# Dilated attention and gated linear attention block on one core: the rest transpose put into the bank of the fourth turned tile, the low-rank weights loaded during gk, and four smaller edits

## The chip, the cores and the metric

The kernel runs on one core of a Trainium2 chip. Time is device microseconds (us) of one execution, the median of 3 runs; lower is better. In tables of the profile, PE is the matrix engine, PEld its weight loads, DVE the vector engine, ACT the scalar engine, POOL the GpSimd engine and SP the engine that only issues DMAs here.

## What is computed

One layer over 512 tokens of width 2048, in float32. An adaLN-modulated RMSNorm gives `h`. One projection of `h` is cut into attention q, k, v and gate, and into q, k, v, gate and low-rank decay inputs of a gated linear attention (GLA):

```python
h = rms_norm(x) * (1.0 + scale[:, None]) + shift[:, None]
proj = h @ w_in[layer]
aq, ak, av, ag, gq, gk, gv, gg, lr_f, lr_b = jnp.split(proj, PROJ_SPLITS, axis=-1)
for window, dilation in DILATED_PATTERNS:        # (128,1), (512,4), (2048,16); 16 heads x 64
    o_p, lse_p = dilated_window_attention(aq, ak, av, rel_bias, window, dilation)
...
att = jnp.einsum('pbsh,pbshe->bshe', mix_w.astype(av.dtype), jnp.stack(outs, axis=0))
a_out = att.reshape(B, S, ATT_WIDTH) * jax.nn.silu(ag)
log_g_f = (jax.nn.log_sigmoid((lr_f @ gla_gate_up_fwd[layer] + ...)) / GLA_GATE_NORM).reshape(ks_)
o_fwd = gla_chunked(gq, gk, gv, log_g_f)         # and o_bwd on flipped inputs; 4 heads, dk 128, dv 256
g_out = rms_norm(o_fwd + o_bwd) * gla_norm_gain * silu(gg)
y = jnp.concatenate([a_out, g_out], axis=-1) @ w_out[layer]
x = x + gate[:, None] * y                        # then rms_norm(x) * final_gain
```

## The kernel before

**Products.** Every large product of float32 numbers is made of three products of rounded ones: each operand is split into a high part (rounded to fp32r, by ACT) and a low part (the difference, by DVE), and PE multiplies high by high, low by high and high by low (`three`, L229 to L232). The work is a sequence of *units*: `sta` and `stb` (L591 on: the first projections), `qk2`, `qk4`, `qk6` and `gk` (64 product steps of three matmuls of 512 columns each), `V` (the GLA values, by seven block products), `ag0`, `ag1`, `gg0`, `gg1` (gates), and the output projection `O` (seven block products, twice). Weights come by DMA from SP into raw tiles and are split as above (`split_hi` L493, `split_lo` L477).

**Order.** PE's order is the program's order, since its queue is scheduled by hand. A unit takes a list of side jobs, pairs of a fraction and a function; a job is emitted when the unit's product steps reach that fraction. DVE, ACT, POOL and SP are ordered by the scheduler, which makes each wait for the last instruction that used the same tile. All engines run their own queue strictly in that order.

**The front.** Before `sta` the condition is spread by eight products (`pc`), and PE then runs bridging products whose results nobody uses: `warm(n)` (L293 to L296) multiplies a tile of ones, `warm(5)` at the start and `warm(6)` behind the spread.

**Attention.** Side jobs of `qk2`, `qk4`, `qk6` and `gk`: four heads in each unit, four query tiles a head. `score(h, i)` (L829) makes two products into a bank `s{h}{i}`, adds the bias and finds the maximum (DVE, L847), takes exponentials (ACT, L851), a reciprocal (DVE, L854) and scales the row (POOL, L864). The probabilities then have to be transposed: `turn(h, i)` (L868) makes three PE transposes of 128x128 into a bank `t{h}{i}` (L882), whose result is split into `pth` (ACT, L888) and `ptl` (DVE, L889). Each query tile has 416 keys, three blocks of 128 and a rest of 32; the four rests of a head lie together in 128 columns of the head's first tile and are turned at once by `rest(h)` (L896): one PE transpose (L899), whose four strips of 32 partitions go to four places of `pth` and `ptl` by four ACT copies (L906) and four DVE subtractions (L908), in two pairs. `rest(h)` is called by `turn(h, 3)`, ahead of its three transposes. `values(h)` (L910) multiplies by v, nine matmuls into a bank `o{h}` (L915).

**PSUM.** There are eight banks of 512 float32 columns: a ring of five, `PJ` (L214), and a ring of three, `PA` (L217). A unit holds four of the `PJ` banks for its products. The fifth is shared by `r{h}`, the turned rests, and `o{h}`; the `PA` banks are taken in turn by `s{h}{i}` and `t{h}{i}`.

**Behind attention.** The low-rank weights are loaded into `lrb` (L1303) and split into `lrs` (ACT L1306, DVE L1307) behind the unit `gk`; their sixteen pairs of products run in the unit `V`. One GLA head each runs beside `V`, `ag0`, `ag1` and `gg0` (`gla_head`, L1012): `gates`, `turn` (three transposes, `kt`, L1062), `states` (three products `kv`, L1074), `att`, `outs` (`go`, L1123) and `norm`, at the fractions `GLA_AT`, or `GLA_FIRST` for head 0. Behind `gg1`, DVE combines blocks of the gated results for the output stage, `to_s1` and `to_s2` (L1471, L1474). The output stage loads half its raw weight tiles into a pool of its own (`out_tile`, L394).

Of the kernel before, what the change touches and what calls it, by code (L numbers as in the profile page):

```python
# [10 lines left out]
F32 = mybir.dt.float32  # L11
# [7 lines left out]
P = 128  # L19
S = 512  # L20
D = 2048
KT = D // P
# [95 lines left out]
REST_OF = (14, 11, 2, 15)  # L118
TOKENS = [slice(256 * c + a, 256 * c + 256, 2) for a in range(2) for c in range(2)]

GLA_AT = (0.01, 0.02, 0.33, 0.46, 0.46, 0.56, 0.64, 0.76, 0.76, 0.88)
GLA_FIRST = (0.3, 0.38, 0.55, 0.62, 0.775, 0.81, 0.86, 0.9, 0.92, 0.97)

SUMS_IN = {"ag0": 8, "ag1": 8, "gg0": 8}

# [66 lines left out]
def block_kernel(ctx: ExitStack, tc: tile.TileContext, a: dict):  # L192
    nc = tc.nc
# [14 lines left out]
    def T2(name, dt=F32, parts=P):  # L208
        return t2.tile([parts, 512], dt, tag="t2", name=name)
# [4 lines left out]
    def PJ(name):  # L214
        return pp.tile([P, 512], F32, tag="pj", bufs=5, name=name)

    def PA(name):  # L217
        return pp.tile([P, 512], F32, tag="pa", bufs=3, name=name)
# [74 lines left out]
    def warm(n):  # L293

        for _ in range(n):
            mm(psw, hot[:, :P], hot, start=True, stop=True)  # L296
# [4 lines left out]
    with tc.manual_schedule(engines=PLANNED):  # L301
        small_inputs()
        cond_load(0, 0)
        half_load(0)
        x_load(0)
        half_load(1)
        nc.scalar.preload_act_table_set("silu_and_others")
        nc.vector.memset(hot.bitcast(F32), 1.0)
        nc.vector.memset(epst, EPS)
        nc.vector.memset(ch.bitcast(F32), 0.0)  # L310
        nc.vector.memset(sel.bitcast(F32), 0.0)
        nc.gpsimd.memset(cl.bitcast(F32), 0.0)
        warm(5)

        nc.vector.tensor_copy(ch[:4], cin[:, :512])
        act(sel[:4], cin[:, 512:], AF.Copy)
        tt(cl[:4], cin[:, :512], ch[:4].bitcast(F32), op=ALU.subtract)

        nc.vector.tensor_scalar(bcond[:, 16:32], bcond[:, 16:32], 1.0, None, op0=ALU.add)
        for j in range(4):  # L320
            spread(j, ch, True)
            spread(j, cl, False)
            act(sb[:, 512 * j:512 * j + 512], pcs[j], AF.Silu)
        warm(6)

    def cond_sum(dst, w, with_, init):

# [65 lines left out]

    def out_tile(s, name):  # L394
        if s % 2 and s >= OUT_DEEP:
            return op.tile([P, 2, 512], F32, tag="raw", bufs=3, name=name)
        return RAW(name, [2, 512])

    second = {}
# [418 lines left out]
    def attention(pairs):  # L818
# [49 lines left out]
        def turn(h, i):  # L868
            def go():
                if not pts:  # L870
                    for z in "hl":
                        pts.append(B8(f"pt{z}", [16, P], F32R))
                        for at, to in ((2, 3), (11, 12)) + ((14, 16),) * (z == "h"):
                            nc.gpsimd.memset(pts[-1][:, at:to, :].bitcast(F32), 0.0)
                if i == 3:
                    rest(h)
                t = pr_.pop((h, i)) if i else pr_[h, i]
                pk = PA(f"t{h}{i}")
                first_ = 0 if i % 2 else 128
                for n_, (c, _) in enumerate(FULL[i]):  # L880
                    kt = (c - i - 1) % 4
                    nc.tensor.transpose(pk[:, n_ * P:n_ * P + P], t[:, first_ + kt * P:first_ + kt * P + P], ident)  # L882
                at, step = FULL[i][0][1], FULL[i][1][1] - FULL[i][0][1]
                hi, lo = (pt[:, at:at + 2 * step + 1:step, :] for pt in pts)
                src = pk[:, :3 * P].rearrange("p (k q) -> p k q", k=3)

                def parts():
                    act(hi, src, AF.Copy)  # L888
                    tt(lo, src, hi.bitcast(F32), op=ALU.subtract)  # L889
                if i or h == heads[0]:  # L890
                    parts()
                else:
                    held_parts.append(parts)
            return go

        def rest(h):  # L896

            pk = PJ(f"r{h}")
            nc.tensor.transpose(pk[:, :P], pr_.pop((h, 0))[:, 0:128], ident)  # L899
            hi, lo = pts  # L900
            to = [(hi, 0, hi, 32), (hi, 0, lo, 0), (hi, 96, lo, 96), (hi, 64, hi, 96)]
            parts = [(t[a:a + 32, REST_OF[i], :], u[b:b + 32, REST_OF[i], :], pk[96 - 32 * i:128 - 32 * i, :P])
                     for i, (t, a, u, b) in enumerate(to)]
            for pair in (parts[:2], parts[2:]):
                for up, _, of in pair:
                    act(up, of, AF.Copy)  # L906
                for up, low_, of in pair:
                    tt(low_, of, up.bitcast(F32), op=ALU.subtract)  # L908
# [103 lines left out]
    def gla_head(h):  # L1012
# [4 lines left out]
        def gates(d):  # L1017
            def go():
                n = f"{h}{d}"
                bias = gbias[:, 4 * d + h:4 * d + h + 1]  # L1020
                pz = PA("z" + n)
                mm(pz, gla["up"][:, d, h * P:h * P + P], gla["lr"], start=True, stop=True)
                e = T2("e" + n)
                act(e, pz, AF.Abs, bias=bias)
                act(e, e, AF.Exp, scale=-1.0)
                act(e, e, AF.Ln, bias=1.0)
                g = T2("g" + n)
                nc.vector.tensor_scalar(g, pz, bias, 0.0, op0=ALU.add, op1=ALU.min)  # L1028
                tt(g, g, e, op=ALU.subtract)
                b = T2("b" + n)  # L1030
                rst = gla["rst"]
                if d == 0:
                    nc.vector.tensor_tensor_scan(b, rst, g, 0.0, op0=ALU.mult, op1=ALU.add)
                    im, il = 63, 127
                else:
                    nc.vector.tensor_tensor_scan(b[:, ::-1], rst, g[:, ::-1], 0.0,
                                                 op0=ALU.mult, op1=ALU.add)
                    im, il = 64, 0
                b3 = b.rearrange("p (n t) -> p n t", n=4)
                sc = gs.tile([P, 3, 4], F32, tag="sc", name="sc" + n, bufs=4)  # L1040
                act(sc[:, 0, :], b3[:, :, im], AF.Exp, scale=1.0 / 16)
                act(sc[:, 1, :], b3[:, :, il], AF.Exp, scale=1.0 / 16)
                bm = T2("bm" + n)
                bm3 = bm.rearrange("p (n t) -> p n t", n=4)
                tt(bm3, b3, b3[:, :, im:im + 1].to_broadcast([P, 4, P]), op=ALU.subtract)
                act(sc[:, 2, :], bm3[:, :, il], AF.Exp, scale=1.0 / 16)
                qi = T2("qi" + n)
                ki = T2("ki" + n)
                act(ki, bm, AF.Exp, scale=-1.0 / 16)
                act(qi, bm, AF.Exp, scale=1.0 / 16)  # L1050
                gq, gk = gla["q"][:, h, :], gla["k"][:, h, :]
                tt(ki, ki, gk, op=ALU.mult)
                tt(qi, qi, gq, op=ALU.mult)
                dirs[d].update(qi=qi, ki=ki, sc=sc, order=[0, 1, 2] if d == 0 else [3, 2, 1])
            return go

        def turn(d):
            def go():
                n, x = f"{h}{d}", dirs[d]
                pk = PA("kt" + n)  # L1060
                for j, c in enumerate(x["order"]):
                    nc.tensor.transpose(pk[:, j * P:j * P + P], x["ki"][:, c * P:c * P + P], ident)  # L1062
                x["kit"] = T2("kit" + n)
                act(x["kit"][:, :384], pk[:, :384], AF.Copy)
            return go
# [65 lines left out]
        def norm():  # L1131
# [10 lines left out]
            for v in range(2):  # L1142
                m = 2 * h + v
                if m % 4 == 0:
# [2 lines left out]
                    op0=ALU.mult, op1=ALU.mult)  # L1147

        at = GLA_AT if h else GLA_FIRST
        return list(zip(at, [gates(0), gates(1), turn(0), turn(1), states(0), states(1), att,  # L1150
                             outs(0), outs(1), norm]))

    def urgent(go):
# [137 lines left out]
        for q in range(2):  # L1291
            qk_evict(p + 2 + q, ps[2 * q], ps[2 * q + 1])

    ps = unit("gk", False, attention((6, 7)))
    kp_.close()
    gs = mid.enter_context(tc.tile_pool(name="gs", bufs=1, reuse_waits="tile"))
    gla["k"] = B8("gkt", [4, 512])
# [1 line left out]
        act(gla["k"][:, i, :], ps[i], AF.Copy)  # L1299


    lrb = T2("lrb")
    nc.sync.dma_start(lrb.rearrange("p (k c) -> p k c", k=KT), a["w_lr"][0])  # L1303
    lrs = gp.tile([P, KT, 2, 32], F32R, tag="g", name="lrs")
    lrb3 = lrb.rearrange("p (k c) -> p k c", k=KT)
    act(lrs[:, :, 0, :], lrb3, AF.Copy)  # L1306
    tt(lrs[:, :, 1, :], lrb3, lrs[:, :, 0, :].bitcast(F32), op=ALU.subtract)  # L1307
    plr = PA("plr")
# [161 lines left out]
    def to_s1(z):  # L1470
        tt(part(z, 1), part(2 + z, 1), part(z, 1), op=ALU.subtract)  # L1471

    def to_s2(z):
        stt(part(z, 0), part(z, 1), -1.0, part(z, 0), op0=ALU.mult, op1=ALU.subtract)  # L1474
# [6 lines left out]
            (0.65, lambda: to_s1(0)), (0.8, lambda: to_s2(0))]  # L1481
    ps = unit("gg1", False, side + some_sums("gg1"))
    gate_evict(ps, cat[3], "g1")
    to_s1(1)
    to_s2(1)
    mid.close()
    op = ctx.enter_context(tc.tile_pool(name="op", bufs=1, reuse_waits="tile"))
    for e in "hl":
# [145 lines left out]
    def later(pair, prod, g, go):  # L1634
        todo.setdefault((pair, prod, g), []).append(go)
# [37 lines left out]
    for z in range(2):  # L1673
        later(0, "P4", 1 + 2 * z, lambda z=z: halves("A12", z, part(2 + z, 0))())
    later(0, "P1", 1, gate_row)
    later(0, "P4", 2, gain_rows(0))
    later(0, "P4", 3, x_again(0))
    later(1, "P7", 0, x_again(1))
# [129 lines left out]
```

## Time and profile before

| | |
|---|---|
| median of 3 runs | 905.07 us (904.97 to 905.77) |
| the profiled execution | 907.22 us, span 905.4 us, mean granted PE clock 0.996 |
| busy share of the span | PE 98%, PEld 82%, DVE 81%, ACT 54%, POOL 14% |
| DMA | 242.33 MB, mean 268 GB/s |

The profile is of one execution. A page of it gives busy times by engine, the chain of work that ended last and the costliest groups of instructions; the trace behind it can be asked for one engine's waits, for the instructions in a stretch of time, and for the busy times of all engines in given stretches, with the clock that PE was granted there (1.00 is full speed).

### The profile page before, as it was taken

Reading aid. Unit: us, or ns where it says so; the run is one execution under the profiler, and the core shown is the slowest. Engines: PE = TensorE matmul, PEld = TensorE weight load, DVE = VectorE, ACT = ScalarE, POOL = GpSimd, SP = SyncE. Lnnn points to the kernel's source line nnn. Section 1 sums busy time; section 2 is a strip of 40 time slices with the busy share of each in tenths; the row PEclk is TensorE's granted clock in tenths of the full one; section 3 lists DMA queues with packets and bytes.
Section 4 is the critical chain, followed back from the end, with each engine's and each line's share of the span. In section 5 each row is a group of like instructions: output and inputs, shape, how many; then the busy total and the mean of one; then the engine's idle time right before and its main releaser. Section 6 shows DMA issues by size and latency. Waiting matters only on the chain.

```text
span 905.4 us, 12339 instructions
## 1 busy us (share of the span) xinstructions
PE 890.0 (98%) x4159; PEld 739.2 (82%) x4159; DVE 731.2 (81%) x1220; ACT 491.6 (54%) x841; POOL 125.9 (14%) x219
## 2 busy tenths in 40 slices
PE   8999999999999999999999999999999999999996
PEld 6888788888888888887778888888888888888885
DVE  7998799878989989888568668595787559797687
ACT  5554533466655745655657554373664248455454
POOL 0000000023323333243000101112020100000001
PEclk9999999999999999999999999999999999999999
DMA  9999489398798898998778879778796988777863
GB/s 342 401 411 363 186 344 367 134 306 226 202 266 273 247 265 247 249 298 223 232 260 255 311 206 308 206 249 262 231 279 208 275 286 289 282 288 249 289 238 154
DMA packets 65547, 242.33 MB, mean 268 GB/s; under 512 B 9190, under 2 KB 11526, under 8 KB 55883
## 3 DMA queue, kind: packets, MB, share of 16 engines
q1 hardware_dynamic: 58724, 199.23, 61.5%
q0 software_dynamic: 6464, 42.01, 19.4%
q8 instruction: 33, 0.54, 0.2%
q10 hardware_dynamic: 296, 0.30, 0.1%
q14 instruction: 30, 0.25, 0.1%
HBM read 224.64 MB, written 51.47 MB: 305 GB/s over the span
## 4 chain that ended last, share of the span: by engine, by line
PE 91%; DVE 3%; ACT 2%; DMA 2%; issue 1%; SPq 0%; DVEq 0%; ACTq 0%
PE ps_qk L230 5%; PE ps_qk L232 5%; PE ps_qk L231 5%; PE g L232 4%; PE g L230 4%; PE g L231 4%; PE stb L232 3%; PE stb L231 3%; PE stb L230 3%; PE ps_ag L232 3%; PE ps_ag L230 3%; PE ps_ag L231 3%; PE o L915 3%; PE sta L230 3%; PE sta L231 3%; PE sta L232 3%
## 5 line engine op out<-in xcount | busy, mean ns | idle before, releaser
L864 POOL TENSOR_SCALAR p<-p,st 128x32 f32<-128x32 f32 (+2 forms) x108 | 59.8, 565 | 159.9 <-DVE st L854 91.2
L328 DVE CUSTOM_DVE_ANT_0 cb<-cb,sb,c_bcond 128x2048 f32<-128x2048 f32 (+1 forms) x32 | 73.4, 2295 | 1.9 <-DMA cb<-in_wm 1.6
L851 ACT ACTIVATE p<-p,st 128x416 f32<-128x416 f32 x64 | 41.0, 641 | 49.2 <-DVE st L847 42.3
L429 POOL DMA_DIRECT2D T<-in_w_o x32 | 23.2, 725 | 159.4 <-ACT V2h L493 14.8
L888 ACT ACTIVATE pth<-t 128x384 fp32r<-128x384 f32 x64 | 31.0, 485 | 19.8 <-PE t L882 11.1
L889 DVE TENSOR_TENSOR ptl<-t,pth 128x384 fp32r<-128x384 f32 x64 | 35.2, 551 | 5.2 <-ACT pth L888 3.7
L882 PE MATMUL t<-c_ident,p 128*128 128x128 f32 x192 | 31.3, 272 | 0.0
L882 PEld LDWEIGHTS t<-c_ident,p 128*128 128x128 f32 x192 | 24.3, 139 | 7.9
L847 DVE CUSTOM_DVE_ANT_0 p<-s,g,st 128x256 f32<-128x256 f32 x64 | 27.7, 432 | 1.8
L847 DVE CUSTOM_DVE_ANT_0 p<-s,g 128x160 f32<-128x160 f32 x64 | 23.5, 367 | 4.2 <-PE s L840 3.5
L328 DVE CUSTOM_DVE_ANT_0 rawg<-rawg,crow,gate 128x1024 f32<-128x1024 f32 x16 | 20.4, 1279 | 4.0 <-DMA rawg<-in_wg 4.0
L1581 POOL TENSOR_SCALAR x<-x,rn 128x512 f32<-128x512 f32 x2 | 2.3, 1167 | 148.5 <-ACT rn L1570 148.5
L429 POOL DMA_DIRECT2D T3V<-in_w_gv x8 | 5.5, 687 | 125.1 <-ACT qk21h L493 118.7
L839 PE MATMUL s<-ks,qh 128*128 128x416 f32 x64 | 22.6, 353 | 0.0
L906 ACT ACTIVATE pth<-r 32x128 fp32r<-32x128 f32 x64 | 17.2, 269 | 9.9 <-PE r L899 4.5
L840 PE MATMUL s<-ks,ql 128*128 128x416 f32 x64 | 22.4, 350 | 0.0
L1091 ACT ACTIVATE sq<-st,sc 128x256 f32<-128x256 f32 x24 | 12.2, 506 | 18.6 <-DVE st L1081 10.0
L328 DVE CUSTOM_DVE_ANT_0 rawg<-rawg,crow,c_bcond 128x1024 f32<-128x1024 f32 x16 | 20.3, 1279 | 0.5 <-DVE g L1028 0.5
L429 POOL DMA_DIRECT2D T<-T x16 | 9.1, 571 | 79.9 <-ACT V8h L493 12.9
L915 PE MATMUL o<-pth,vv 128*128 128x512 f32 (+1 forms) x64 | 15.9, 369 | 2.2 <-DVE pth L908 1.1
L466 DVE TENSOR_TENSOR raw_O<-raw_O,raw_P 128x1024 f32<-128x1024 f32 x8 | 9.8, 1225 | 10.1 <-DMA raw_O<-in_w_o 7.8
L568 ACT ACTIVATE h_hi<-xt,shift 128x512 fp32r<-128x512 f32 x16 | 11.5, 721 | 10.3 <-DVE shift L328 9.5
(1661 smaller groups left out, 3151.6 us busy)
## 6 DMA issues: line engine op xcount, KB each, us to landing
cb<-in_wm SPq DMA_DIRECT2D x31, 1024.0 KB, 9.3
T<-in_w_o POOLq DMA_DIRECT2D x32, 512.0 KB, 6.5
rawg<-in_wg SPq DMA_DIRECT2D x32, 512.0 KB, 5.4
raw_O<-in_w_o SPq DMA_DIRECT2D x32, 512.0 KB, 4.6
raw_qk<-in_w_qk SPq DMA_DIRECT2D x24, 512.0 KB, 4.9
raw_O<-T SPq DMA_DIRECT2D x24, 512.0 KB, 5.0
rawb<-in_w_sb SPq DMA_DIRECT2D x16, 512.0 KB, 8.9
rawv<-in_wv SPq DMA_DIRECT2D x16, 512.0 KB, 5.6
```

Of the source, the lines that this page charges most:

```text
L230: mm(ps, lh, rh, start=first, stop=False, skip_group_check=more)
L231: mm(ps, ll, rh, start=False, stop=False, skip_group_check=more)
L232: mm(ps, lh, rl, start=False, stop=last, skip_group_check=more)
L328: return nc.vector.tensor_tensor_reduce(out=w, in0=w, in1=with_, op0=ALU.mult, op1=ALU.add, scale=1.0, scalar=init, accum_out=dst)
L429: move = nc.gpsimd.dma_start(dst, src, max_dma_last_dim=8192, **how).ins
L847: top = nc.vector.tensor_tensor_reduce(out=t[:, lo:hi], in0=ps[:, lo:hi], in1=gt[h][:, at:at + 2 * (hi - lo) - 1:2], op0=ALU.add, op1=ALU.min,
L851: act(t, t, AF.Exp, bias=st[:, 0:1], scale=-1.0, accum_out=st[:, 1:2])
L864: last["pool"] = nc.gpsimd.tensor_scalar(to, of, st[:, 2:3], 1.0, op0=ALU.mult, op1=ALU.mult).ins
L882: nc.tensor.transpose(pk[:, n_ * P:n_ * P + P], t[:, first_ + kt * P:first_ + kt * P + P], ident)
L888: act(hi, src, AF.Copy)
L889: tt(lo, src, hi.bitcast(F32), op=ALU.subtract)
L915: mm(po[:, P * a0:P * a1], vv[h // 4][:, c, h % 4, :], pt[:, at:at + (a1 - a0 - 1) * step + 1:step, :], start=n_ == z == 0, stop=False, sk ...
```

## The change

Six edits:

1. `rest` writes its transpose into the last quarter of the bank `t{h}3`, which `turn(h, 3)` now takes first; the bank `r{h}` is no longer used. The code's order stays: the rest's transpose, its eight evictions, then the three transposes of the tile.
2. `lrb` is loaded by a side job of `gk` at 0.7 in place of behind `gk`.
3. The bridging products behind the spread are thirteen in place of six.
4. In a GLA head, `states(0)` comes ahead of `turn(1)`, whose fraction is 0.47 in place of 0.46; for head 0 the two `outs` come at 0.91 and 0.93 in place of 0.90 and 0.92.
5. `to_s1(1)` and `to_s2(1)` are emitted within the first block product of the output stage, in place of ahead of it.
6. The output stage's own raw tiles are four in place of three.

```diff
-GLA_AT = (0.01, 0.02, 0.33, 0.46, 0.46, 0.56, 0.64, 0.76, 0.76, 0.88)
-GLA_FIRST = (0.3, 0.38, 0.55, 0.62, 0.775, 0.81, 0.86, 0.9, 0.92, 0.97)
+GLA_AT = (0.01, 0.02, 0.33, 0.46, 0.47, 0.56, 0.64, 0.76, 0.76, 0.88)
+GLA_FIRST = (0.3, 0.38, 0.55, 0.775, 0.62, 0.81, 0.86, 0.91, 0.93, 0.97)
...
-        warm(6)
+        warm(13)
...
-            return op.tile([P, 2, 512], F32, tag="raw", bufs=3, name=name)
+            return op.tile([P, 2, 512], F32, tag="raw", bufs=4, name=name)
...
+                pk = PA(f"t{h}{i}")
                 if i == 3:
-                    rest(h)
+                    rest(h, pk[:, 3 * P:])
                 t = pr_.pop((h, i)) if i else pr_[h, i]
-                pk = PA(f"t{h}{i}")
...
-        def rest(h):
-
-            pk = PJ(f"r{h}")
-            nc.tensor.transpose(pk[:, :P], pr_.pop((h, 0))[:, 0:128], ident)
+        def rest(h, pk):
+
+            nc.tensor.transpose(pk, pr_.pop((h, 0))[:, 0:128], ident)
...
-            parts = [(t[a:a + 32, REST_OF[i], :], u[b:b + 32, REST_OF[i], :], pk[96 - 32 * i:128 - 32 * i, :P])
+            parts = [(t[a:a + 32, REST_OF[i], :], u[b:b + 32, REST_OF[i], :], pk[96 - 32 * i:128 - 32 * i, :])
...
-        return list(zip(at, [gates(0), gates(1), turn(0), turn(1), states(0), states(1), att,
+        return list(zip(at, [gates(0), gates(1), turn(0), states(0), turn(1), states(1), att,
                              outs(0), outs(1), norm]))
...
-    ps = unit("gk", False, attention((6, 7)))
+    def lr_load():
+        lrb.append(T2("lrb"))
+        nc.sync.dma_start(lrb[0].rearrange("p (k c) -> p k c", k=KT), a["w_lr"][0])
+
+    ps = unit("gk", False, attention((6, 7)) + [(0.7, lr_load)])
...
-    to_s1(1)
-    to_s2(1)
...
+    later(0, "P1", 1, lambda: (to_s1(1), to_s2(1)))
```

What the edits do to the order on the engines shows best at two places. The first is PE in the unit `gk`, at head 12's rest and fourth turned tile; `ps_gk` are the unit's products, `p` the probabilities, and a number behind a name tells one buffer from another. The brackets name the engines' counters that the instruction waits for. Before:

```order
L232 MATMUL ps_gk_3671<-h_lo,gk3h 128x512
L899 MATMUL r_3894<-c_ident,p_3734 128x128 [waits Pool_49]
L882 MATMUL t_3904<-c_ident,p_3817 128x128 [waits DVE_49,PE_49,Activation_49]
L882 MATMUL t_3904<-c_ident,p_3817 128x128 x2
L230 MATMUL ps_gk_3672<-h_hi,gk3h 128x512
```

And after:

```order
L232 MATMUL ps_gk_3666<-h_lo,gk3h 128x512
L898 MATMUL t_3889<-c_ident,p_3729 128x128 [waits DVE_49,PE_49,Pool_49]
L882 MATMUL t_3889<-c_ident,p_3812 128x128 [waits DVE_49,Activation_49]
L882 MATMUL t_3889<-c_ident,p_3812 128x128 x2
L230 MATMUL ps_gk_3667<-h_hi,gk3h 128x512
```

The sequence of PE's work is the same, but the rest's transpose now writes the tile of the three that follow, and it is the rest's transpose that waits for the bank's former users. The count of DVE's counter for which the first of the three waits is, after, that of the last of the four rest subtractions of the same head (L907 there); this is so in all 16 heads. Before, it was that of an earlier user of the bank `t`.

The second place is DVE's queue in the same head. Before:

```order
L854 RECIPROCAL st_3873<-st_3873 128x1 [waits Activation_49]
L908 TENSOR_TENSOR pth<-r_3894,pth 32x128 [waits PE_49,Activation_49]
L908 TENSOR_TENSOR ptl<-r_3894,pth 32x128
L889 TENSOR_TENSOR ptl<-t_3904,pth 128x3x128 [waits Activation_49]
L847 ISA p_3916,st_3917<-s_3913,g_3751 128x160 [waits PE_49,Pool_49]
L847 ISA st_3917 128x1
L908 TENSOR_TENSOR ptl<-r_3894,pth 32x128 [waits Activation_49]
L847 ISA p_3916,st_3917<-s_3913,g_3751,st_3917 128x256 [waits DVE_49]
L847 ISA st_3917 128x1
L908 TENSOR_TENSOR pth<-r_3894,pth 32x128
```

And after:

```order
L854 RECIPROCAL st_3868<-st_3868 128x1 [waits Activation_49]
L907 TENSOR_TENSOR pth<-t_3889,pth 32x128 [waits PE_49,Activation_49]
L907 TENSOR_TENSOR ptl<-t_3889,pth 32x128
L907 TENSOR_TENSOR ptl<-t_3889,pth 32x128 [waits Activation_49]
L907 TENSOR_TENSOR pth<-t_3889,pth 32x128
L889 TENSOR_TENSOR ptl<-t_3889,pth 128x3x128 [waits Activation_49]
```

The four subtractions of the rest now stand together, ahead of that of the three blocks (L889) and of the next tile's bias; on ACT the four copies stand together in the same way. The third place is ACT's queue where the low-rank weights are split. Before, in head 15:

```order
L906 ACTIVATE pth<-r_4296 32x128 [waits PE_49]
L906 ACTIVATE pth<-r_4296 32x128
L1306 ACTIVATE lrs<-lrb 128x16x32 [waits DMAHW3_49,DMAHW2_49]
L888 ACTIVATE pth<-t_4306 128x3x128 [waits PE_49]
L906 ACTIVATE pth<-r_4296 32x128 [waits DVE_49]
```

And after, where it stands between heads 14 and 15:

```order
L888 ACTIVATE pth<-t_4124 128x3x128 [waits PE_49,Activation_49]
L1309 ACTIVATE lrs<-lrb 128x16x32 [waits DMAHW6_49,DMAHW3_49]
L493 ACTIVATE V0h<-raw_V_4069 128x1024 [waits PE_49]
L851 ACTIVATE p_4138,st_4139<-p_4138,st_4139 128x416 [waits DMAHW1_49,DVE_49,Pool_49]
```

The split of the low-rank weights has moved ahead by most of a head. Its load on SP moved with it, from behind the load of `raw_V6` to just behind that of `raw_V4`. POOL's order is the same; `to_s1(1)` and `to_s2(1)` stand on DVE where the scheduler had put them before.

More of the change, by code (lines that the diff above doesn't have):

```diff
@@ L1292, in block_kernel @@
             qk_evict(p + 2 + q, ps[2 * q], ps[2 * q + 1])
-    ps = unit("gk", False, attention((6, 7)))
+    lrb = []
+    def lr_load():
+        lrb.append(T2("lrb"))
+        nc.sync.dma_start(lrb[0].rearrange("p (k c) -> p k c", k=KT), a["w_lr"][0])
+    ps = unit("gk", False, attention((6, 7)) + [(0.7, lr_load)])
     kp_.close()
@@ L1299, in block_kernel @@
         act(gla["k"][:, i, :], ps[i], AF.Copy)
-    lrb = T2("lrb")
-    nc.sync.dma_start(lrb.rearrange("p (k c) -> p k c", k=KT), a["w_lr"][0])
     lrs = gp.tile([P, KT, 2, 32], F32R, tag="g", name="lrs")
-    lrb3 = lrb.rearrange("p (k c) -> p k c", k=KT)
+    lrb3 = lrb[0].rearrange("p (k c) -> p k c", k=KT)
     act(lrs[:, :, 0, :], lrb3, AF.Copy)
```

## Prediction

> **What bounds the kernel now.** I read the page first, then PE's waits, then the busy times of stretches with the granted clock, and last the timeline at the places that the change touches.
>
> ```profile
> span 905.4 us, 12339 instructions
> PE 890.0 (98%) x4159; PEld 739.2 (82%) x4159; DVE 731.2 (81%) x1220; ACT 491.6 (54%) x841; POOL 125.9 (14%) x219
> PE 91%; DVE 3%; ACT 2%; DMA 2%; issue 1%; SPq 0%; DVEq 0%; ACTq 0%
> ```
>
> PE is busy for 98% of the span and makes 91% of the chain that ended last. So a microsecond in which PE stands still is a microsecond of the whole, and work on DVE or ACT counts only where PE waits for it. PE's waits are few:
>
> ```profile
> PE sta L591 <- ACT h_hi L534: 2.7, 1, 2.7
> PE o L915 <- DVE pth L908: 1.1, 1, 1.1
> PE o L915 <- ACT pth L888: 1.0, 1, 1.0
> ```
>
> The columns are the total, how often and the longest. In attention PE waits at two places only; the rest of the time the products of the unit hide everything, as the windows show (PE, PEld, DVE, ACT and POOL busy, then clock):
>
> ```profile
> 7.87:11.28 3.41, 1.03 (x5) 0.84 (x6) 2.81 (x6) 2.23 (x5) 0.00 (x0) 1.00 1.03 407
> 11.28:14.69 3.41, 3.41 (x10) 2.64 (x9) 2.31 (x3) 1.00 (x2) 0.00 (x0) 0.50 1.03 429
> 14.69:18.10 3.41, 3.41 (x16) 2.82 (x15) 3.04 (x6) 2.00 (x4) 0.00 (x0) 1.00 1.01 408
> ...
> 257.00:315.00 58.00, 58.00 (x290) 48.79 (x289) 52.74 (x148) 35.59 (x82) 20.48 (x36) 1.00 0.86 266
> 416.20:419.61 3.41, 2.31 (x12) 1.76 (x11) 3.27 (x12) 0.87 (x3) 1.08 (x2) 1.00 1.03 161
> 440.00:443.41 3.41, 2.40 (x11) 1.70 (x10) 1.54 (x4) 2.19 (x6) 0.00 (x0) 1.00 0.38 158
> ```
>
> From 257 to 315 PE is busy all 58.00 us. The first two rows show what idle PE time costs beside itself: after a window of 3.41 us with 1.03 busy, the next window ran at half clock, and then full again. Windows with 2.31 and 2.40 busy were not followed by a drop.
>
> **The rest in the turned tile's bank.** This decides. Head 12 in the trace, rest and what follows it:
>
> ```profile
> 398.35 0.27 PE L899 MATMUL r<-c_ident,p 128*128 128x128 f32 x1
> 398.46 0.49 PE L882 MATMUL t<-c_ident,p 128*128 128x128 f32 x3
> 399.00 0.55 ACT L906 ACTIVATE pth<-r 32x128 fp32r<-32x128 f32 x2
> 399.59 0.29 DVE L908 TENSOR_TENSOR pth<-r,pth 32x128 fp32r<-32x128 f32 x1
> 399.90 0.28 DVE L908 TENSOR_TENSOR ptl<-r,pth 32x128 fp32r<-32x128 f32 x1
> 400.22 0.56 ACT L906 ACTIVATE pth<-r 32x128 fp32r<-32x128 f32 x2
> 401.04 0.29 DVE L908 TENSOR_TENSOR ptl<-r,pth 32x128 fp32r<-32x128 f32 x1
> 401.89 0.28 DVE L908 TENSOR_TENSOR pth<-r,pth 32x128 fp32r<-32x128 f32 x1
> ```
>
> Here the three transposes L882 start 0.11 us after the rest's, while its evictions run until 402.17 behind PE's back. In the changed order the same three write the bank that holds the rest, and the first of them waits for the last of the four subtractions. PE runs in order: behind the waiting transpose stand all products of the unit, so nothing hides the wait. It happens in each of the 16 heads.
>
> How long is it? The shortest chain is built from rows. An ACT that is free starts 0.30 after the transpose:
>
> ```profile
> 426.41 0.27 PE L899 MATMUL r<-c_ident,p 128*128 128x128 f32 x1
> ...
> 426.71 0.57 ACT L906 ACTIVATE pth<-r 32x128 fp32r<-32x128 f32 x2 [0.83 <-PE r L899]
> ```
>
> A pair of copies and the step to DVE take 0.59 (399.00 to 399.59), a pair of subtractions and the step back 0.63 (399.59 to 400.22), then again 0.59 and 0.59 (0.29 + 0.02 + 0.28). PE's wake-up behind such a subtraction, and the wait of the first `o`, are in these rows:
>
> ```profile
> 416.82 0.40 PE L232 MATMUL ps_gk<-h_lo,gk5h 128*128 128x512 f32 x1
> 417.89 0.28 DVE L908 TENSOR_TENSOR pth<-r,pth 32x128 fp32r<-32x128 f32 x1
> 418.32 0.88 PE L915 MATMUL o<-pth,vv 128*128 128x512 f32 x3 [1.10 <-DVE pth L908]
> ```
>
> The subtraction ends at 418.17 and PE starts at 418.32, 0.15 later. Together 0.30 + 0.59 + 0.63 + 0.59 + 0.59 + 0.15 = 2.85, less the 0.11 that PE spends anyway: 2.74 per head, 43.8 for 16. To that comes what stands ahead on ACT and DVE. In head 12 the first copy started 0.65 after the transpose, 0.35 later than at 426.71, as ACT was in an exponential; I take that for the mean head and 0.2 (an estimate, about the reciprocal of 0.15 that DVE does ahead of the first pair) for DVE. So 3.29 a head, **53**. Upper bound: if the evictions stay as spread as in head 12 now (402.17 − 398.35 = 3.82, less 0.11, plus 0.15), 3.86 a head and 61.8.
>
> [...]
>
> **The clock.** A stall of 3.3 us leaves its mark in the windows. A window of 3.41 with 2.38 idle dropped the clock; windows with 1.10 and 1.01 idle did not; in between the trace is silent. If stalls fall anywhere against the windows, the chance that one window holds at least 2.38 of 3.3 idle is (3.41 + 3.3 − 2 × 2.38) / 3.41 = 0.57, and that it holds 1.10 is 1. So 9 to 16 windows at half clock. What one costs the front shows:
>
> ```profile
> 10.25 1.21 PE L591 MATMUL sta<-sa0hi,h_hi 128*128 128x512 f32 x4 [2.65 <-ACT h_hi L534]
> ...
> 14.68 1.09 PE L591 MATMUL sta<-sa0hi,h_hi 128*128 128x512 f32 x4
> ...
> 15.55 0.94 ACT L534 ACTIVATE h_hi<-xt,scale 128x256 fp32r<-128x256 f32 x2
> ...
> 17.44 1.07 PE L591 MATMUL sta<-sa1hi,h_hi 128*128 128x512 f32 x4
> ```
>
> Twelve products take 4.43 (10.25 to 14.68) and the next twelve 2.76 (0.23 each): 1.6 to 1.7 lost. I take 10 windows, near the lower end, since only the row with 2.38 idle shows a drop: **16** (0 to 25.6).
>
> [...]
>
> **Thirteen bridging products.** Seven more at 0.23 are 1.6 us, into the 2.65 idle ahead of `sta`. That window then holds about 2.4 busy in place of 1.03, above the 2.31 that did no harm, so the half clock at 11.28 goes and 24 products end by 15.8. The next needs `h_hi` of the second slice, which ACT ends at 16.49: it starts at 16.55 and not at 17.44, **−0.9** (0 if the clock falls all the same).
>
> **The waits for o.** Rests are done before `t`'s own evictions, so `o` waits for them no more. The one above, 418.32 less 416.82 and 0.23, is **−1.27**.
>
> **The low-rank load.** Now:
>
> ```profile
> 434.49 0.64 SPq L1303 DMA_DIRECT2D lrb<-in_w_lr  x1
> ...
> 441.12 0.63 ACT L1306 ACTIVATE lrs<-lrb 128x512 fp32r<-128x512 f32 x1 [2.78 <-DMA lrb<-in_w_lr]
> ...
> 440.92 0.39 PE L232 MATMUL ps_gv_P<-V0l,h_hi 128*128 128x512 f32 x1
> 442.31 1.13 PE L915 MATMUL o<-pth,vv 128*128 128x512 f32 x4 [1.01 <-ACT pth L888]
> ```
>
> ACT waits for the load with head 15's `pth` behind it, and PE loses 442.31 − 440.92 − 0.23 = **−1.16**, which goes. The split now stands ahead of `V0h` and head 15's first exponential on ACT, its subtraction amid that head's bias on DVE. The load takes 6.6 us from issue, and is issued behind `raw_V4` on SP, near 418 in the old time, so it lands near 424.5, about when that place is reached. It may hold both queues by 0 to 1.5; I take **+0.5**. The SP loads behind it move by one issue (0.6), fetched well ahead: 0.
>
> **The GLA order and the output stage.** Two waits that a little more distance covers:
>
> ```profile
> 524.46 0.39 PE L232 MATMUL ps_gv_P<-V25l,vS 128*128 128x512 f32 x1
> 525.13 0.46 PE L1123 MATMUL go<-at,gv 128*128 128x128 f32 x2 [0.28 <-ACT V27h L493]
> ...
> 666.86 0.39 PE L232 MATMUL ps_gg<-h_lo,gg03h 128*128 128x512 f32 x1
> 667.38 0.55 PE L1062 MATMUL kt<-c_ident,ki 128*128 128x128 f32 x3
> ```
>
> 0.67 − 0.23 = 0.44 and 0.52 − 0.23 = 0.29: three or more products come between, so **−0.7**; at worst a new wait of the same size elsewhere, 0. `to_s1` and the fourth raw tile change no order that PE waits for: 0, and if the output stage's loads bunch, some tenths.
>
> **The sum.** 907.2 (the profiled execution, whose span is 905.4) + 53 + 16 − 0.9 − 1.27 − 1.16 − 0.7 + 0.5 = 972.7. That execution lies 2.15 above the median of the runs, so **970.5**.
>
> **The rivals.**
> - *Stalls without the clock.* The gaps are too short or cut in two by the windows. For it: the windows with about 1 us idle; against it: the front. 970.5 − 16 = 954.5. Chance 0.25.
> - *The wait is covered.* The last subtraction is done before PE's transpose is ready to start, so that only the gains are left: 907.2 − 3.5 − 2.15 = 901.5. It decides if stalls stay under 3.5 / 16 = 0.22 us a head. Against it: the evictions cannot begin before the rest's transpose, and the next one follows 0.11 behind. Chance 0.03; between that and no change 0.02.
> - *A longer chain.* Evictions as spread as now and a drop in every head, 61.8 + 25.6 for 53 + 16: 989 and more. Chance 0.1.
>
> The forecast has 0.6. The range is from the shortest chain without the clock, 907.2 + 43.8 − 3.5 − 2.15 = 945, to the third rival, 989: it takes in the first rival and leaves out the ends. A measurement tells about 0.2% (1.8 us) from no change: faster 0.03, within it 0.02, slower 0.95.
>
> **What would show it.** PE's waits should list the transposes L882 waiting for DVE's L907, 16 times, 2.7 to 3.9 us each, 44 to 62 together, PE's busy share near 92 to 93%, and after each a chance of a window at 0.50, 10 or so. The waits of `o` should be gone and that of `sta` near 1.1. If the 16 waits are there at full clock, the first rival holds; if PE shows no wait at L882, my reading of the wait is wrong.

## The result and the profile after

The changed kernel takes 989.3 us (median of 6 runs, 984.76 to 990.24) against 905.66 us before (6 runs, 904.97 to 906.37): a ratio of 1.0917, 95% interval 1.0896 to 1.0938. Its profiled execution took 990.24 us, with a span of 988.5 against 905.4. The page of the kernel after begins:

```profile
span 988.5 us, 12368 instructions
PE 920.8 (93%) x4166; PEld 762.0 (77%) x4166; DVE 734.2 (74%) x1220; ACT 493.5 (50%) x841; POOL 122.0 (12%) x219
PEclk9999999999799889899899999999999999999999
```

Two things carry the 83.1 us of span. PE's idle time rose from 905.4 − 890.0 = 15.4 to 988.5 − 920.8 = 67.7, by 52.3. And PE's busy time rose by 30.8 with seven matmuls more: the same matmuls took longer, and the third line says where, in slices of the attention units. PE's waits in the trace after (total, times, longest) explain the first:

```profile
PE t L882 <- DVE pth L907: 54.9, 16, 4.2
PE kv L1073 <- ACT kit L1063: 2.6, 1, 2.6
PE warm L296 <- DVE hot L308: 1.5, 1, 1.5
```

54.9 + 2.6 came; the old waits of `sta` (2.7), `o` (2.1) and `go` (0.3) went: 52.4 of 52.3. The second line is a new wait, which the prediction had only as an "at worst". Here is head 12 again, rows of the timeline after; the rest's transpose is now L898:

```profile
461.07 0.27 PE L898 MATMUL t<-c_ident,p 128*128 128x128 f32 x1
461.72 0.56 ACT L905 ACTIVATE pth<-t 32x128 fp32r<-32x128 f32 x2
462.04 0.15 DVE L854 RECIPROCAL st<-st 128x1 f32<-128x1 f32 x1
462.32 0.29 DVE L907 TENSOR_TENSOR pth<-t,pth 32x128 fp32r<-32x128 f32 x1
462.63 0.28 DVE L907 TENSOR_TENSOR ptl<-t,pth 32x128 fp32r<-32x128 f32 x1
462.95 0.55 ACT L905 ACTIVATE pth<-t 32x128 fp32r<-32x128 f32 x2 [0.66 <-DVE ptl L907]
463.53 0.29 DVE L907 TENSOR_TENSOR ptl<-t,pth 32x128 fp32r<-32x128 f32 x1 [0.62 <-ACT pth L905]
463.83 0.28 DVE L907 TENSOR_TENSOR pth<-t,pth 32x128 fp32r<-32x128 f32 x1
464.26 0.52 PE L882 MATMUL t<-c_ident,p 128*128 128x128 f32 x3 [2.92 <-DVE pth L907]
```

Before, L882 came 0.11 behind the rest's transpose; now it comes 3.19 behind it, 0.15 after the fourth subtraction has ended. Each step of the chain is there: copies, subtractions, copies, subtractions, wake-up.

The clock is read in windows of 3.41 us, the length of the single half-clock stretches in this trace (columns: length, PE, PEld, DVE, ACT and POOL busy, PE clock, DMA share, GB/s):

```profile
225.83:229.25 3.42, 0.58 (x5) 0.25 (x4) 1.80 (x6) 1.73 (x6) 0.85 (x2) 1.00 0.60 230
229.25:232.66 3.41, 3.41 (x11) 2.90 (x11) 1.19 (x4) 1.55 (x2) 0.00 (x0) 0.50 0.02 5
232.66:236.07 3.41, 3.41 (x19) 2.84 (x18) 2.84 (x10) 0.74 (x2) 1.25 (x3) 1.00 0.14 19
242.90:246.31 3.41, 0.96 (x5) 0.52 (x3) 3.02 (x11) 1.60 (x6) 1.75 (x3) 1.00 0.54 171
246.31:249.73 3.42, 2.27 (x7) 2.01 (x8) 1.13 (x3) 0.86 (x3) 0.45 (x2) 0.50 0.65 110
249.73:253.14 3.41, 3.41 (x11) 2.69 (x11) 1.38 (x5) 0.47 (x1) 0.00 (x0) 0.50 0.13 26
...
205.35:522.79 317.44, 262.52 (x1152) 216.70 (x1151) 207.76 (x559) 145.30 (x324) 71.45 (x133) 0.89 0.66 187
```

The stall of head 1 leaves 0.58 busy in its window, and the next runs at half clock: 11 matmuls there, 19 in the one behind. Head 2's stall reaches over two windows, and two half-clock windows follow. Over the 93 windows of the last row the mean clock was 0.89; 0.11 × 93 × 2 is 20 half-clock windows, and the clock's records list the same 20: they follow the stalls of 14 of the 16 heads, six of them with two windows.

### The profile page after: what moved, and what is told of

It is laid out like the page before. It is cut to its first block, busy times and chain, and to the rows that moved or that the text cites. A ratio compares the mean times of both kernels' runs of the same rounds, so it can differ in the third digit from the quotient of the medians.

```text
span 988.5 us, 12368 instructions
## 1 busy us (share of the span) xinstructions
PE 920.8 (93%) x4166; PEld 762.0 (77%) x4166; DVE 734.2 (74%) x1220; ACT 493.5 (50%) x841; POOL 122.0 (12%) x219
## 4 chain that ended last, share of the span: by engine, by line
PE 84%; DVE 8%; ACT 5%; issue 2%; POOL 0%; DVEq 0%; ACTq 0%; POOLq 0%
PE ps_qk L230 4%; PE ps_qk L231 4%; PE ps_qk L232 4%; PE g L232 4%; PE g L230 3%; PE g L231 3%; PE stb L232 3%; PE stb L231 3%; PE stb L230 3%; PE ps_ag L232 3%; PE ps_ag L230 3%; PE ps_ag L231 3%; PE ps_gv_P L231 3%; PE ps_gv_P L230 3%; PE ps_gv_P L232 3%; PE sta L230 3%
## 5 line engine op out<-in xcount | busy, mean ns | idle before, releaser
L882 PE MATMUL t<-c_ident,p 128*128 128x128 f32 x192 | 36.5, 305 | 54.9 <-DVE pth L907 54.9
L864 POOL TENSOR_SCALAR p<-p,st 128x32 f32<-128x32 f32 (+2 forms) x108 | 55.1, 518 | 238.4 <-DVE st L854 123.2
L882 PEld LDWEIGHTS t<-c_ident,p 128*128 128x128 f32 x192 | 26.8, 157 | 67.6 <-ACT pth L905 53.2
L889 DVE TENSOR_TENSOR ptl<-t,pth 128x384 fp32r<-128x384 f32 x64 | 35.4, 553 | 32.2 <-ACT pth L888 29.7
L905 ACT ACTIVATE pth<-t 32x128 fp32r<-32x128 f32 x64 | 17.1, 268 | 16.6 <-DVE ptl L907 10.8
L1358 DVE TENSOR_TENSOR vS<-rawS,vS 128x1024 fp32r<-128x1024 f32 x8 | 9.7, 1222 | 8.7 <-ACT vS L1357 8.5
L1122 PE MATMUL go<-qi,sq 128*128 128x128 f32 x96 | 15.9, 275 | 0.0
```

The lines of the kernel that those rows point to most:

```text
L864: last["pool"] = nc.gpsimd.tensor_scalar(to, of, st[:, 2:3], 1.0, op0=ALU.mult, op1=ALU.mult).ins
```

## The experiments

Ten kernels ran. Times are medians; the kernel before, run beside them on the same chip, had 905.16, 905.24 and 905.95 in the three sets (15, 15 and 23 runs). Gaps that the expectations call stand-still are counted between PE's starts, so they hold the 2.6 us that the waits' list leaves out while the rest's transpose itself counts as busy.

**The rest in its own bank again.** All of the change but the first edit:

```diff
-                    rest(h, pk[:, 3 * P:])
+                    rest(h)
...
+            pk = PJ(f"r{h}")
```

> All of the change but the first edit: the rest has its own bank again. If the wait of the transposes for the rest's last subtraction and the clock that it costs are nearly all of the loss (57.5 us of standing still and some 29 us of half clock by the gaps between PE's starts in the trace after), the time is that of the kernel before with the five small edits: 905.7 - 0.9 (front) - 1.2 (low-rank load) - 0.7 (go, kt) + 2.7 (new wait of kv in the last gate unit with a GLA head) = 905.6, within 903.5 to 907. Rival: the other edits carry a good part of the loss (a low-rank split that holds ACT and DVE, the later output loads): 910 or more. PE should show no wait at the transposes, clock 0.99 or more.

908.01 us (9 runs), a ratio of 1.003 (1.0018 to 1.0041): the first edit carries all of the loss but 2.8 us, 81.3 of 84.1 by these medians. The 2.8 is 1 us above the range that I gave for this run. PE's waits:

```profile
PE kv L1074 <- ACT kit L1064: 2.6, 1, 2.6
PE warm L296 <- DVE hot L308: 1.5, 1, 1.5
PE sta L591 <- ACT h_hi L534: 1.1, 1, 1.1
PE o L915 <- DVE pth L908: 1.1, 1, 1.1
```

The transposes wait no more, one old wait of `o` is back, and kv's is there. What the expectation had left out is the clock behind kv's wait in this execution:

```profile
671.08:674.50 3.42, 0.96 (x4) 0.87 (x5) 1.11 (x2) 0.92 (x3) 1.44 (x2) 1.00 0.87 337
674.50:677.91 3.41, 3.41 (x9) 2.66 (x8) 1.45 (x3) 1.36 (x3) 0.95 (x2) 0.50 0.34 131
```

One half-clock window, some 1.6 us more, an estimate from the front of the kernel before, where twelve products took 4.43 in place of 2.76.

**The first edit alone**, on the kernel before:

```diff
-                    rest(h)
+                    rest(h, pk[:, 3 * P:])
```

> The kernel before with the first edit alone. If the costs add up, it is the kernel after less what the five others cost together (908.0 - 905.2 = 2.8): 986.5, within 982 to 990, with 16 waits of the transposes, 54 to 58 us. Rival: the late low-rank split of the kernel before adds to a head's stall, or the other edits brought part of the stalls: outside 982 to 990.

985.57 us (4 runs; 1.0886, 1.0870 to 1.0902), with 16 waits of 54.1 us. The costs add up: 80.3 alone, 81.3 within the whole.

**Unused products in the gap.** This parts the standing still from the clock. PE is given work that depends on nothing:

```diff
                     rest(h, pk[:, 3 * P:])
+                    pf = PJ(f"fill{h}")
+                    for _ in range(12):
+                        mm(pf, onesr, h_hi[:, 0, :], start=True, stop=True)
```

> The whole change, and between the rest's transpose and the three that wait, twelve products of 512 columns that nobody uses (2.7 us of PE work in each of the 16 heads). If the drops of the clock come from PE's idle time, the stand-still costs the same 57 us (2.7 of 3.6 a head filled, some 0.9 left as wait, 14 us in all) but the clock stays at 1.00 in attention: 989.3 - 29 = 960, within 955 to 965. Rival: the drops have another cause (the many transposes, or the load on the chip), or the filling delays the evictions: 985 or more. A second rival, that the clock cost nothing and the stall all: also 989.

964.31 us (4 runs; 1.0650, 1.0633 to 1.0668). The gap itself did not shrink; head 12 in its timeline:

```profile
439.90 0.27 PE L901 MATMUL t<-c_ident,p 128*128 128x128 f32 x1
439.93 3.01 PE L880 MATMUL fill<-h_hi,ones 128*128 128x512 f32 x12
443.10 0.52 PE L885 MATMUL t<-c_ident,p 128*128 128x128 f32 x3 [0.16 <-DVE pth L910]
```

3.20 from rest to tile, as with the gap empty (3.19). But the clock held: 0.99 over the attention units against 0.89, one half-clock window in place of 20. So 25.0 us of the loss are the clock's; this is a little less than the 20 windows cost, since the profiled execution with the products still has that one window and another behind kv's wait. (The products' results are used by nothing.)

**Five in place of twelve**, so that less of the gap is idle than in the kernel after, and more than with twelve:

> The whole change with five unused products (1.1 us) in place of twelve between the rest's transpose and the three that wait, so some 2.45 us a head are left idle. By the trace after, a window of 3.41 us is followed by half clock if about 2.03 or more of it is idle. Then about (3.41 + 2.45 - 4.06) / 3.41 = 0.53 of the heads drop, 8 or 9 and a few of them for two windows, some 13 us: 989 - 29 + 13 = 973, within 966 to 981. If the limit lies near 1.1 us idle, all heads drop as before: 988. If only a nearly whole idle window counts (3 us or more), none: 964.

973.13 us (4 runs; 1.0753, 1.0729 to 1.0777), 10 half-clock windows (the mean clock was 0.95 over the attention units), as the middle case expected. Two windows of it, each with the one behind it:

```profile
259.75:263.16 3.41, 1.30 (x7) 1.15 (x8) 2.09 (x7) 1.23 (x4) 0.00 (x0) 1.00 1.04 229
263.16:266.58 3.42, 3.42 (x9) 2.65 (x8) 2.20 (x4) 2.21 (x4) 0.00 (x0) 0.50 1.00 232
454.31:457.72 3.41, 1.64 (x10) 1.10 (x9) 1.41 (x7) 1.29 (x4) 1.32 (x3) 1.00 0.96 353
457.72:461.14 3.42, 3.42 (x19) 2.94 (x18) 2.63 (x9) 0.74 (x2) 0.53 (x1) 1.00 0.80 331
```

1.30 busy was followed by half clock, 1.64 was not.

**Four transposes together, then the evictions.** The bank is shared as in the change, only the order differs:

```diff
                 if i == 3:
-                    rest(h, pk[:, 3 * P:])
+                    nc.tensor.transpose(pk[:, 3 * P:], pr_.pop((h, 0))[:, 0:128], ident)
...
+                if i == 3:
+                    rest(h, pk[:, 3 * P:])
```

> The whole change, but the rest's transpose and the tile's three are made one after the other into the shared bank, and all evictions come behind them. If the order of transposes and evictions is the cause, the wait is gone although the bank is shared: 903.9 (905.6 as with its own bank, less the 1.7 that o waited for late rest evictions), within 902 to 908, no wait at the transposes. Rival: sharing the bank itself costs (the three banks of the ring are held longer, or the evictions of one bank hold each other up until o waits): 915 or more, with waits at s, t or o in most heads.

917.71 us (4 runs; 1.0139, 1.0125 to 1.0154). Each side has a part: the 16 waits are gone, so it was the order of transposes and evictions that cost 71.6 of the 81.3. But the time is the rival's: in this order the shared bank is not free. PE's waits in attention, the largest first:

```profile
PE o L915 <- ACT pth L890: 4.2, 6, 1.6
...
PE o L915 <- DVE ptl L891: 1.5, 3, 0.6
```

`s` waits too, three times, 1.7 in all. Together this is 7.4, where `o` waits 1.1 with the own bank, and so accounts for 6.3 of the 9.7 us between the two kernels; where the rest comes from stays open. In head 15 ACT's second pair of copies from that bank waits 0.45 for DVE, DVE's next subtraction then 0.61 for that pair, and on ACT other work (0.60 and 1.05) stands ahead of the copy of the tile. The end of ACT's part of head 15 in the timeline, down to the copy of the tile:

```profile
447.80 0.55 ACT L906 ACTIVATE pth<-t 32x128 fp32r<-32x128 f32 x2 [0.45 <-DVE ptl L908]
448.37 0.60 ACT L1305 ACTIVATE gkt<-ps_gk 128x512 f32<-128x512 f32 x1
448.86 1.05 ACT L493 ACTIVATE V2h<-raw_V 128x1024 fp32r<-128x1024 f32 x1
449.81 0.48 ACT L890 ACTIVATE pth<-t 128x384 fp32r<-128x384 f32 x1
...
450.35 0.91 PE L915 MATMUL o<-pth,vv 128*128 128x512 f32 x3 [1.61 <-ACT pth L890]
```

**The same, the tile's blocks evicted first:**

> As with the four transposes made together in the shared bank, but the three blocks of the tile are evicted first and the rest's strips after them. If ACT and DVE have to take turns on the bank whatever the order, the chain stays as long and o now waits for the rest's last copy: 912, within 908 to 919. Rival: it mattered only that the big eviction came last, so that the cost of sharing goes: 904 to 908.

910.50 us (4 runs; 1.0059, 1.0045 to 1.0073): within the range given, but the chain that the expectation named has a small part in it. `o` waits for the rest's copies 1.2 in all, about as long as it waits with the own bank (1.1), and `s` waits once, 2.0. That one wait comes from the low-rank load:

```profile
423.98 0.63 ACT L1310 ACTIVATE lrs<-lrb 128x512 fp32r<-128x512 f32 x1 [4.36 <-DMA lrb<-in_w_lr]
424.52 1.04 ACT L493 ACTIVATE V0h<-raw_V 128x1024 fp32r<-128x1024 f32 x1
...
426.09 0.85 ACT L888 ACTIVATE pth<-t 128x384 fp32r<-128x384 f32 x2
...
426.81 0.54 DVE L889 TENSOR_TENSOR ptl<-t,pth 128x384 fp32r<-128x384 f32 x1
...
427.40 0.46 PE L839 MATMUL s<-ks,qh 128*128 128x416 f32 x1 [1.99 <-DVE ptl L889]
```

ACT stands 4.36 us in front of the split until its load lands, the evictions of the tiles turned meanwhile come behind it, and PE waits for their bank. A half-clock window follows. So the 2.5 between this kernel and the own bank (908.01) are not shown to be a cost of sharing: the trace puts this wait and the window on the low-rank load. No kernel without the moved load was run in this order. One of the three waits of `s` in the kernel before this one, 1.0, has the same chain.

**The GLA order alone**, on the kernel before:

```diff
-        return list(zip(at, [gates(0), gates(1), turn(0), turn(1), states(0), states(1), att,
+        return list(zip(at, [gates(0), gates(1), turn(0), states(0), turn(1), states(1), att,
```

with the fractions of the change.

> The kernel before with the fourth edit alone (order and fractions of the GLA heads). By the trace after, kv of the second direction waits 2.7 us in the last gate unit that has a head, since ACT's copy of kt now stands behind the scaled states of the first direction: 905.7 + 2.7 - 0.4 (go) - 0.3 (kt) = 907.7, within 906.5 to 909. Rival, as predicted: only the two small waits go, 905.0.

908.13 us (7 runs; 1.0036, 1.0021 to 1.0051): slower by 3.0, within the range given and not on the predicted side. In its profiled execution (907.28) no half-clock window followed the wait; with the window that followed it in the run with the own bank it would cost 1.6 more, so the median may hold both kinds. Its ACT queue in `gg0`:

```profile
667.76 0.51 ACT L1091 ACTIVATE sq<-st,sc 128x256 f32<-128x256 f32 x1 [0.73 <-DVE st L1081]
...
669.76 0.51 ACT L1091 ACTIVATE sq<-st,sc 128x256 f32<-128x256 f32 x1 [0.54 <-DVE st L1086]
671.76 0.51 ACT L1091 ACTIVATE sq<-st,sc 128x256 f32<-128x256 f32 x1 [1.49 <-DVE st L1086]
672.17 0.47 ACT L1064 ACTIVATE kit<-kt 128x384 f32<-128x384 f32 x1
```

The copy of the second direction's transposes stands behind three scaled states of the first, each of which waits for a step of DVE's chain, and PE's `kv` stands still for it.

**The other small edits.** Thirteen bridging products alone, and the low-rank load alone, on the kernel before:

> The kernel before with thirteen bridging products in place of six, alone. As predicted: 0.9 us less (904.3 against 905.2), with sta's wait near 1.1 us in place of 2.7 and no half-clock window behind it. Rival: the window after the front drops only in some executions of the kernel before (where the windows happen to hold the gap whole), so that little is gained: within 0.4 us of the kernel before.

905.14 us (12 runs; 0.9988, 0.9979 to 0.9998), 0.8 less than the kernel before in the same set (905.95), though `sta`'s wait was still 1.5. The size is the predicted one, but the absolute time, 904.3, was missed: in the two other sets the kernel before had 905.2. And the rival's mechanism is in the traces: the three other profiled kernels with six products (`sta` waits 1.7 to 1.9) have no half-clock window behind the front. So the window seems to come in some executions only, the profiled one of the kernel before among them.

> The kernel before with the low-rank load at 0.7 of gk, alone. As predicted: o's wait behind ACT's low-rank split goes, -1.2 us, and at most 0.5 comes back where the split now stands: 904.0 to 904.6 against 905.2. Rival: the split waits for its load in the new place and holds up head 15's first tile: no gain, 905 to 906.

905.10 us (12 runs; 0.9989, 0.9979 to 0.9998), 0.85 less than in the same set, and again in absolute time the rival's (905 to 906). `o`'s wait behind the split is gone. ACT's wait for the load is not: it is 1.0 in place of 2.8, and 1.7 with the own bank, where in both PE does not notice it. In the kernel after, whose attention takes longer, the split finds its load landed.

**The version without the two that cost:** the own bank and the old GLA order, the other edits kept.

> The whole change but the first edit and the order of the GLA heads (the later fractions of head 0's outs stay). If the 2.7 us wait of kv and the half-clock window behind it are what made the other five edits cost 2.7 us together, they go: 908.0 - 2.7 - 1.6 + 0.3 (kt's old wait) = 904.0, about 1 below the kernel before, within 902 to 905. Rival: the low-rank load or the later output loads cost too, so that the time stays at 906 or more.

904.27 us (11 runs; 0.9987, 0.9978 to 0.9996): it beats both kernels, the one before by 1.0 us (0.4 to 2.0 by the interval).

## Why the prediction was right, and where its sizes were off

- **The place and the sign** were right: PE stands still in each head from the rest's transpose to the last rest subtraction, 16 times, and nothing hides it. The own bank takes it away, the first edit alone brings it.
- **The stall**, 53, measured 54.9 by the waits' list, 57.5 counted as in the sum (16 × 0.16 more). Head 12 was 3.19 − 0.11 against 3.29. The heads were uneven: the longest, head 14, waited 4.2, since there the rest's subtractions stand on DVE among the next tile's bias steps and another tensor operation (L1251, 0.69): the second starts 1.35 behind the first, where 0.31 would do. The prediction had 0.2 for such work.
- **The clock** is the step that was mis-sized: 16 predicted from 10 windows, against 20 windows that cost 25.0 us by the filled gap (PE's busy time grew by 30.8 in all). Two things failed. I took the limit to be near the one row with a drop (1.03 busy of 3.41), while windows with up to 1.51 busy were followed by half clock; by the formula of the prediction with 1.9 idle that is 0.85 of the heads, close to the 14 of 16 seen. And I counted one window a head, while in six heads a half-clock window that itself held part of the stall (1.56 to 2.64 busy) was followed by another. The first rival, a stall without the clock, is refuted by the filled gap: 25.0 us went with the idle time alone. Length alone does not tell: half clock followed five of the six stalls of 2.8 to 2.9 in the kernel after, and the one wait of 2.0 in the kernel that evicts the tile's blocks first.
- **The GLA order** failed in sign: −0.7 predicted, with a new wait named only as an "at worst" that would bring the term to 0; alone it costs 3.0. I followed PE's queue, where more products come between, and not ACT's, where the copy that kv needs moved behind a chain.
- **The small gains** are of the predicted size, the front 0.8 against 0.9, the low-rank load 0.85 against 1.16 − 0.5, but both with intervals of about 0.9 to either side, and against a kernel before whose median moved by as much from set to set. The front's term was in part counted twice: the sum takes 0.9 off the profiled execution, which had the half-clock window, and then 2.15 to come to the median. In the trace after, `o`'s waits are gone.
- **The sum.** By the own-bank run the first edit costs 81.3, where the prediction's terms for it (53 + 16 − 1.27) make 67.7, and the five others cost 2.8, where theirs make −2.3. These two misses, 13.6 and 5.1, are nearly all of the 18.8 between 970.5 and 989.3.
- The measured time lies at the very end of the range, which was set by the third rival (989 and more). Half of that rival came true, the drop in nearly every head (25.0, against its 25.6); the chain did not get as long as its 61.8, and the five other edits made up the difference. That the range still reaches this time is in part luck: it left no room for a loss by the small edits. The output stage's edits were not tried alone; the version with them and without the two costly edits is 1.0 faster than the kernel before, so no large loss can lie there.

That the wait is necessary is not shown: no kernel here lets PE write the bank while its strips are read. What the runs show is that the order of issue alone, with the same bank, removes it.

## What to carry to other kernels

Before putting a second result into a bank that is being filled, write down the order of writes and evictions: here a write that came behind an eviction of the same bank waited for it, and everything behind it on PE waited too (54.9 us in 16 heads). Emit all writes to a bank first, and evict the larger part first (910.5 against 917.7 us). Then look at every queue that a moved step touches, not only the bottleneck's, and price idle time of the matrix engine with the clock that it costs afterwards, here 25.0 us on top of the 54.9.

## What the runs showed of the hardware

The 15 half-clock stretches in the trace of the kernel after, 3.41 or 6.83 us long up to the last product, begin at multiples of 3.41 us from each other (212.18, 229.25, 246.31 and so on); this gives the bounds of the windows. Two windows of the kernel after, each with the one behind it:

```profile
208.77:212.18 3.41, 1.40 (x8) 1.29 (x9) 1.49 (x6) 1.02 (x3) 0.85 (x2) 1.00 0.76 293
212.18:215.59 3.41, 3.41 (x12) 2.70 (x11) 1.83 (x7) 0.73 (x2) 1.12 (x3) 0.50 0.21 79
311.16:314.58 3.42, 1.54 (x8) 0.95 (x6) 2.70 (x10) 1.66 (x6) 1.43 (x4) 1.00 0.73 236
314.58:317.99 3.41, 2.50 (x15) 2.21 (x16) 1.86 (x6) 1.70 (x3) 0.00 (x0) 1.00 0.46 150
```

The closest pair is a window of the kernel that evicts the tile's blocks first, with 1.51 busy, and another of the kernel after, with 1.52:

```profile
425.49:428.91 3.42, 1.51 (x7) 1.06 (x8) 3.32 (x9) 1.67 (x6) 0.61 (x1) 1.00 0.35 109
428.91:432.32 3.41, 3.41 (x11) 2.81 (x10) 2.65 (x12) 2.71 (x9) 2.16 (x4) 0.50 0.50 187
...
430.63:434.04 3.41, 1.52 (x9) 0.98 (x7) 2.97 (x7) 2.96 (x7) 0.09 (x1) 1.00 1.08 339
434.04:437.46 3.42, 1.75 (x10) 1.52 (x11) 2.00 (x5) 1.46 (x4) 0.00 (x0) 1.00 0.92 230
```

The first of this pair was followed by half clock, the second was not. In the traces of the kernels before and after, one execution of each, the 15 full-clock windows between the first and the last product with at most 1.40 busy were all followed by half clock, and none with 1.52 or more was. So in these traces PE's busy time in such a window parts the two kinds, and the length of a gap does not: the wait of 3.56 us in head 11 of the kernel after, cut in two by the window's end at 434.04, was followed by no half clock, the wait of 2.0 above was. Of the windows already at half clock in the kernel after, those with 1.56 to 2.64 busy were followed by another, those with 2.94 or more by full clock. Its 16 stalls, of 2.8 to 4.2 us, cost no half-clock window in two heads, one in eight and two in six.
